# When and how densely a second list of rows is scattered to DRAM, in a two-layer encoder with product-key experts

## The chip, the cores and the metric

The kernel runs on one core of a Trainium2 chip. The metric is the device time of one execution in microseconds (us). The launch has two layers, and both run the same program on other weights.

## The reference

Each of the two layers adds a token mixer (two kinds of attention, gates, projections) and then a product-key expert layer to `x`, 256 tokens of 1024 numbers. The change touches only the expert layer:

```python
def peer_ffn(x, w_query, sub_keys, expert_down, expert_up):
    ...
        q = (xc @ w_query).reshape(PEER_CHUNK, PEER_HEADS, 2, half)
        s = jnp.einsum('thpk,pnk->thpn', q, sub_keys).astype(jnp.float32)
        sv, si = lax.top_k(s, PEER_TOPK)
        ...
        top_s, sel = lax.top_k(cand, PEER_TOPK)
        eidx = jnp.take_along_axis(cidx, sel, axis=-1)
        g = jax.nn.softmax(top_s, axis=-1)
        u = expert_down[eidx]
        vv = expert_up[eidx]
        act = jax.nn.gelu(jnp.einsum('td,thkd->thk', xc, u).astype(jnp.float32), approximate=False)
        return jnp.einsum('thk,thkd->td', (g * act).astype(x.dtype), vv)
```

Each token uses 8 heads x 16 of the 16,384 experts (128 x 128). The sum over `vv` needs only the rows of `expert_up` that some token uses.

## The kernel before, in words

**Stages of a layer.** Attention and projections come first. Then the expert layer has two long stages on TensorE. In the *downs* stage the kernel multiplies all 16,384 rows of `expert_down` with all 256 tokens: 128 units of 128 experts, two units to a PSUM bank (loop `b` from L1351 on, matmuls L1367 to L1369). Beside it VectorE finds the top 16, and gates are spread into a table `act`, which holds for each of 128 expert rows `i` (128 experts, one per partition) a row of 258 words: the gated activation for two halves of 128 tokens, and behind each half the expert's number. In the *ups* stage TensorE multiplies blocks of 128 rows of `expert_up` with those activations (`block`, matmuls L1401); three matmuls of 128x512 per half of the output and per half of the tokens, as weights and activations are both split into a high and a low part.

**Two lists and eight whole rows.** The expert rows are in three parts. List 1 (`r` = 0) holds the rows 0 to 79. The experts of it that are used are packed into 66 blocks of 128, of which 33 serve both token halves and 33 one half; they alternate. The rows 80 to 87 are taken whole, 8 units, without packing. List 2 (`r` = 1) holds the rows 88 to 127, packed into 33 blocks. The ups stage goes through list 1, the whole rows, list 2, 107 units.

**Packing takes four steps.** `rank_lane` computes each expert's place in its list (VectorE writes `rank`, L1178). `send_lane` then *sends* every row `i` of `act`: an indirect DMA from GpSimd (POOL) scatters its 128 x 258 words to their places in a DRAM table, `rows` (L1212): 80 sends for list 1, 40 for list 2. When all sends of a list are done, `read_back` brings blocks of 128 places back into SBUF by SP (L1243), into a ring of 16. And `rows` starts, from the expert numbers at the end of the block, an indirect DMA from POOL that *gathers* 128 rows of `expert_up`, 512 KB (L1272). The whole rows are loaded directly by SP (L1269).

**What a gathered unit passes through.** ScalarE copies it, rounded, to `wh` (L199), VectorE subtracts that from the original into `wl` (L203, the *split* of the unit, whose name is put in the list `st.splits`), and TensorE uses both. The raw buffers are a ring of `DEEP` = 10: 4 `raw`, 6 within `act`. A gather of unit n needs the split of unit n - 10; `wh` and `wl` have 4 buffers, so the split of unit n needs TensorE to be done with unit n - 4.

**What sets the order.** The kernel's Python simulates clocks of the engines (`Lanes`) and records instructions in the order in which lanes become ready; every engine then works its queue in that order. POOL and SP queues are in order too, so a send that waits holds back each gather behind it. `st.nd` counts the loads recorded so far, `up0` is the number of the layer's first ups unit, and `whole` is that of the first whole row.

**Pacing.** Each send is given a dependence on one entry of `st.splits`, so that the sends spread out in time: `pace` starts three entries before the end of the list and moves on by a step per send. While `pace` is past the end, the lane waits in the recording, up to 15 steps of 0.2 us of its own clock. For list 2 the lane waits besides until the first `DEEP` ups loads are recorded:

```python
            while r and st.nd < up0 + DEEP:
                yield None
            pace = len(st.splits) - 3.0
```

Of the kernel before, what the change touches and what calls it, by code (L numbers as in the profile page):

```python
# [58 lines left out]
DEEP = RAWS + AHEAD  # L59
# [167 lines left out]
def encoder_kernel(ctx, tc, x_in, wts, downs, ups, gains, gate_bias, qk_norm, rpb, sink, skeys, consts, sums, out,  # L227
# [8 lines left out]
    lanes = Lanes()  # L236
# [41 lines left out]
    def lane_need(keys):  # L278
        while not all(k in done for k in keys):
            yield None  # L280
        yield ("at", max(done[k] for k in keys))
# [71 lines left out]
    st = Stream(nc, wpool, srcs, lanes)  # L353
# [121 lines left out]
    for l in range(depth):  # L475
# [719 lines left out]
        def send_lane(r):  # L1195

            i0, w = LISTS[r][:2]
            yield from lane_need([("rank", r)])
            whole = up0 + len([x for x in seq if x[1] == 0])
            while r and st.nd < up0 + DEEP:  # L1200
                yield None
            pace = len(st.splits) - 3.0
            for i in range(i0, i0 + w):
                yield from lane_need([("row", i // 2)])

                tries = 0
                while int(pace) >= len(st.splits) and tries < 15 and lanes.stuck < 5:
                    tries += 1
                    yield ("w", 0.2)
                    yield ("p", 0.0)  # L1210

                snd = nc.gpsimd.indirect_dma_start(byrank[r], bass.IndirectOffsetOnAxis(ap=rank[:, i:i + 1], axis=0),  # L1212
                                                   afl[:, i * ROW:(i + 1) * ROW], None)
                key = f"send{l}{r}"
                if i > i0:
                    tc.declare_no_dep(snd.ins, group=key, reason="places of one list differ")
                tc.add_to_no_dep_group(key, snd.ins)
                tc.add_manual_dep(snd.ins, st.splits[min(int(pace), len(st.splits) - 1)],
                                  mybir.DependencyInfo(mybir.DependencyClass.Sync, mybir.DependencyReason.DATA),
                                  reason="pace")  # L1220

                pace += 0.4 if r == 0 else 1.8 if st.nd < whole else 0.6
                sends[r].append(snd.ins)
                nc.gpsimd.nop()
                yield ("w", 0.8)
                yield ("p", 0.0)
            sent.add((l, r))
            st.load(0)
# [101 lines left out]
        for r in range(len(LISTS)):  # L1330
            lanes.add(send_lane(r))
        stage, ring, sent, sends = {}, {}, set(), {r: [] for r in range(len(LISTS))}
        st.rows = rows
        up0 = u + 12 + 128
# [239 lines left out]
```

## Time and profile before

| | |
|---|---|
| time, median of 3 runs | 1810.36 us (1807.65 to 1810.52) |
| time of the profiled execution | 1814.21 us |
| its span, first to last instruction | 1812.4 us |
| PE busy | 1779.2 us, 98% of the span |
| DVE, ACT, POOL busy | 1439.7, 1096.0, 581.6 us |
| granted clock of PE, mean | 0.998 |
| DMA, mean | 208 GB/s |

The profile is of one execution, which is 3.85 us longer than the median of the runs. The span is 1.8 us shorter than that execution's own time. PE's busy time counts each matmul from its start to its modelled end, and neighbours overlap, so a count of matmuls in a stretch tells more of a pause than the busy time does. In layer 0 the ups stage begins at 673.93 us, in layer 1 at 1578.31 us.

### The profile page before, as it was taken

How to read it: one execution, taken by the hardware profiler on the slowest of the kernel's cores; microseconds unless marked ns; L12 is line 12 of the kernel's file. 1: busy time of each engine (PE TensorE's matmuls, PEld its weight loads, DVE VectorE, ACT ScalarE, POOL GpSimd, SP SyncE). 2: the span in 40 equal slices, each digit the busy share in tenths (PEclk: the TensorE clock that was granted, in tenths of full speed). 3: DMA queues.
4: the chain of work that ended last, by engine and by line, in shares of the span. 5: the costliest groups of instructions: out<-in, count | busy, mean ns of one | idle time of the engine just before them, and what ended most of it. 6: DMA issues, size and time to landing. Idle time of an engine off the chain costs nothing. (4 is left out here: it accounts for less than half of the span.)

```text
span 1812.4 us, 38043 instructions
## 1 busy us (share of the span) xinstructions
PE 1779.2 (98%) x14646; PEld 1632.9 (90%) x14646; DVE 1439.7 (79%) x3278; ACT 1096.0 (60%) x1788; POOL 581.6 (32%) x480
## 2 busy tenths in 40 slices
PE   8999999999999999989999999999999999999998
PEld 7889899999999998768878898999999999988786
DVE  6986799988878867656679867999888788677665
ACT  5675556666667646555656655556666676466554
POOL 0000260000047737775300002500000477377661
PEclk9999999999999999999999999999999999999999
DMA  7535456544468879999654354455444677899893
GB/s 260 161 112 171 150 164 186 165 151 148 147 187 243 244 254 319 297 318 320 215 204 150 110 176 153 156 186 172 148 145 152 187 244 240 262 326 334 307 333 131
DMA packets 130519, 377.42 MB, mean 208 GB/s; under 512 B 17552, under 2 KB 43792, under 8 KB 130320
## 3 DMA queue, kind: packets, MB, share of 16 engines
q1 hardware_dynamic: 90288, 239.28, 43.0%
q0 software_dynamic: 40032, 135.54, 20.8%
q8 instruction: 119, 1.95, 0.5%
q14 instruction: 80, 0.66, 0.1%
HBM read 342.00 MB, written 32.75 MB: 207 GB/s over the span
## 5 line engine op out<-in xcount | busy, mean ns | idle before, releaser
L203 DVE TENSOR_TENSOR wl<-raw,wh 128x1024 fp32r<-128x1024 f32 x444 | 541.6, 1222 | 150.3 <-ACT wh L199 142.2
L199 ACT ACTIVATE wh<-raw 128x1024 fp32r<-128x1024 f32 x476 | 502.5, 1057 | 226.5 <-PE bank L1368 53.8
L1367 PE MATMUL bank<-TT,wh 128*128 128x256 f32 x2048 | 592.0, 289 | 0.0
L1368 PE MATMUL bank<-TT,wh 128*128 128x256 f32 x2048 | 578.9, 283 | 0.0
L1369 PE MATMUL bank<-TT,wl 128*128 128x256 f32 x2048 | 578.4, 282 | 0.0
L1368 PEld LDWEIGHTS bank<-TT,wh 128*128 128x128 f32 x2048 | 392.1, 191 | 0.0
L1369 PEld LDWEIGHTS bank<-TT,wl 128*128 128x128 f32 x2048 | 391.8, 191 | 0.0
L1367 PEld LDWEIGHTS bank<-TT,wh 128*128 128x128 f32 x2048 | 391.5, 191 | 0.3
L1401 PE MATMUL bank<-wh,TT 128*128 128x512 f32 x1296 | 355.1, 393 | 10.6 <-ACT TT L1288 5.5
L1212 POOL DMA_INDIRECT rows<-act,rank x240 | 275.5, 1148 | 98.2 <-issue 61.3
L1401 PEld LDWEIGHTS bank<-wh,TT 128*128 128x128 f32 x1296 | 241.0, 188 | 73.1 <-DVE TT L1290 11.9
L888 POOL IOTA act<- 128x128 uint32 (+2 forms) x6 | 2.0, 332 | 891.7 <-PE bank L368 409.9
L203 DVE TENSOR_TENSOR wl<-act,wh 128x1024 fp32r<-128x1024 f32 x126 | 154.4, 1227 | 82.2 <-ACT wh L199 81.8
L1401 PE MATMUL bank<-wl,TT 128*128 128x512 f32 x648 | 201.6, 390 | 0.7 <-issue 0.7
L199 ACT ACTIVATE wh<-act 128x1024 fp32r<-128x1024 f32 x126 | 133.4, 1060 | 102.5 <-PE bank L1401 76.0
L1272 POOL DMA_INDIRECT act<-in_ups_dram,act x118 | 131.3, 1112 | 72.4 <-DVE TT L1290 27.4
L1401 PEld LDWEIGHTS bank<-wl,TT 128*128 128x128 f32 x648 | 122.0, 188 | 26.8 <-issue 1.1
L448 PE MATMUL bank<-TT,wh 128*128 128x256 f32 x448 | 130.1, 290 | 1.6 <-ACT raw_ka L577 1.0
L450 PE MATMUL bank<-TT,wh 128*128 128x256 f32 x448 | 126.6, 283 | 0.0
L451 PE MATMUL bank<-TT,wl 128*128 128x256 f32 x448 | 126.6, 283 | 0.0
L1272 POOL DMA_INDIRECT raw<-in_ups_dram,act x80 | 95.7, 1197 | 84.7 <-DMA act<-rows 54.6
L1072 ACT ACTIVATE oh<-oh 128x1024 f16<-128x1024 f16 (+2 forms) x108 | 101.4, 955 | 11.5 <-DVE oh L1069 10.4
(268 smaller groups left out, 2898.8 us busy)
## 6 DMA issues: line engine op xcount, KB each, us to landing
raw<-in_downs_dram SPq DMA_DIRECT2D x256, 512.0 KB, 3.8
raw<-in_wts_dram SPq DMA_DIRECT2D x132, 512.0 KB, 4.1
act<-rows SPq DMA_DIRECT2D x100, 129.0 KB, 5.0
act<-rows SPq DMA_DIRECT2D x98, 64.5 KB, 5.9
act<-in_ups_dram SPq DMA_DIRECT2D x8, 512.0 KB, 7.7
raw<-in_ups_dram SPq DMA_DIRECT2D x8, 512.0 KB, 5.3
rows<-act,rank POOLq DMA_INDIRECT x240
act<-in_ups_dram,act POOLq DMA_INDIRECT x118
```

The costliest lines, as they stand in the source:

```text
L199: self.nc.scalar.activation(h, r, AF.Copy)
L203: self.splits.append(engine.tensor_sub(lo, r, h.bitcast(F32)).ins.name)
L448: nc.tensor.matmul(o, wh, rh, start=first and i == 0 and pc == 0, stop=False, skip_group_check=True)
L450: nc.tensor.matmul(o, wh, rl, start=False, stop=False, skip_group_check=True)
L451: nc.tensor.matmul(o, wl, rh, start=False, stop=last and i == len(kcs) - 1 and pc == 1, skip_group_check=True)
L1072: nc.scalar.activation(el, ej, AF.Copy, scale=LOW)
L1212: snd = nc.gpsimd.indirect_dma_start(byrank[r], bass.IndirectOffsetOnAxis(ap=rank[:, i:i + 1], axis=0), afl[:, i * ROW:(i + 1) * ROW], None)
L1272: nc.gpsimd.indirect_dma_start(w, None, ups_rows, bass.IndirectOffsetOnAxis(ap=num, axis=0), element_offset=l * 16384 * D)
L1367: nc.tensor.matmul(o, lh, TT[:, :, 0, kc, :], start=kc == 0, stop=False)
L1368: nc.tensor.matmul(o, lh, TT[:, :, 1, kc, :], start=False, stop=False)
L1369: nc.tensor.matmul(o, ll, TT[:, :, 0, kc, :], start=False, stop=kc == 7)
L1401: nc.tensor.matmul(oacc[ch][hf], a, r[:, hf * 512:(hf + 1) * 512], start=first[hf] and a is lh and r is h, stop=last and a is ll)
```

## The change

It edits `send_lane` alone, and there only list 2:

- The wait until ten ups loads are recorded goes. The lane for list 2 records sends as soon as its places are known.
- `pace` starts six entries before the end of `st.splits`, not three, and a send may be tied at the latest to the fourth entry from the end (`lag` = 4), not to the last.
- The steps: 0.4 per send until two ups loads are recorded, then 2.8 (was 1.8) until the whole rows come, then 0.8 (was 0.6).

For list 1 the values come out as they were.

```diff
--- before.py
+++ after.py
@@ -1197,14 +1197,14 @@
             i0, w = LISTS[r][:2]
             yield from lane_need([("rank", r)])
             whole = up0 + len([x for x in seq if x[1] == 0])
-            while r and st.nd < up0 + DEEP:
-                yield None
-            pace = len(st.splits) - 3.0
+
+            lag = (1, 4)[r]
+            pace = len(st.splits) - (3.0, 6.0)[r]
             for i in range(i0, i0 + w):
                 yield from lane_need([("row", i // 2)])
 
                 tries = 0
-                while int(pace) >= len(st.splits) and tries < 15 and lanes.stuck < 5:
+                while int(pace) > len(st.splits) - lag and tries < 15 and lanes.stuck < 5:
                     tries += 1
                     yield ("w", 0.2)
                     yield ("p", 0.0)
@@ -1215,11 +1215,11 @@
                 if i > i0:
                     tc.declare_no_dep(snd.ins, group=key, reason="places of one list differ")
                 tc.add_to_no_dep_group(key, snd.ins)
-                tc.add_manual_dep(snd.ins, st.splits[min(int(pace), len(st.splits) - 1)],
+                tc.add_manual_dep(snd.ins, st.splits[min(int(pace), len(st.splits) - lag)],
                                   mybir.DependencyInfo(mybir.DependencyClass.Sync, mybir.DependencyReason.DATA),
                                   reason="pace")
 
-                pace += 0.4 if r == 0 else 1.8 if st.nd < whole else 0.6
+                pace += 0.4 if r == 0 or st.nd < up0 + 2 else 2.8 if st.nd < whole else 0.8
                 sends[r].append(snd.ins)
                 nc.gpsimd.nop()
                 yield ("w", 0.8)
```

On TensorE, VectorE and ScalarE the recorded order is the same in both kernels. POOL's queue moves. At the start of layer 0's ups stage it held this, where `rows_2244` is the DRAM table of list 1 and `rows_2245` that of list 2 (a send writes to it), and a DMA from `in_ups_dram` is a gather:

```order
L1212 DMA rows_2244<-act,rank 10240x258 x80
L1272 DMA raw<-in_ups_dram,act 128x1024 x4
L1272 DMA act<-in_ups_dram,act 128x1024 x6
L1272 DMA raw<-in_ups_dram,act 128x1024
L1212 DMA rows_2245<-act,rank 5120x258 x2
L1272 DMA raw<-in_ups_dram,act 128x1024
L1212 DMA rows_2245<-act,rank 5120x258
L1272 DMA raw<-in_ups_dram,act 128x1024 x2
L1272 DMA act<-in_ups_dram,act 128x1024 x2
L1212 DMA rows_2245<-act,rank 5120x258 x2
L1272 DMA act<-in_ups_dram,act 128x1024 x2
L1212 DMA rows_2245<-act,rank 5120x258
```

And now:

```order
L1212 DMA rows_2244<-act,rank 10240x258 x80
L1212 DMA rows_2245<-act,rank 5120x258 x9
L1272 DMA raw<-in_ups_dram,act 128x1024
L1212 DMA rows_2245<-act,rank 5120x258
L1272 DMA raw<-in_ups_dram,act 128x1024
L1212 DMA rows_2245<-act,rank 5120x258 x2
L1272 DMA raw<-in_ups_dram,act 128x1024
L1212 DMA rows_2245<-act,rank 5120x258
L1272 DMA raw<-in_ups_dram,act 128x1024
L1272 DMA act<-in_ups_dram,act 128x1024 x6
L1272 DMA raw<-in_ups_dram,act 128x1024 x2
```

Nine sends of list 2 moved ahead of the first gather, four more stand among the first four gathers, and behind them the sends stand further apart. Counting on to the 66th gather, the last of list 1, 33 sends of list 2 stand before it now and 32 before; seven and eight follow it. Layer 1 has the same counts at these places.

On SP, at the end of list 1 in layer 0, whole rows (L1269), blocks read back (L1243, from `rows_2245` those of list 2) and the next layer's gains (L1448) stood so:

```order
L1243 DMA act<-rows_2244 128x129
L1269 DMA act<-in_ups_dram 128x1024 x4
L1269 DMA raw<-in_ups_dram 128x1024 x2
L1243 DMA act<-rows_2245 128x258
L1243 DMA act<-rows_2245 128x129
L1269 DMA raw<-in_ups_dram 128x1024
L1243 DMA act<-rows_2245 128x258
L1269 DMA raw<-in_ups_dram 128x1024
L1448 DMA act<-in_gains_dram 128x1024
L1243 DMA act<-rows_2245 128x129
L1243 DMA act<-rows_2245 128x258
```

And now:

```order
L1243 DMA act<-rows_2244 128x129
L1269 DMA act<-in_ups_dram 128x1024 x4
L1269 DMA raw<-in_ups_dram 128x1024 x4
L1448 DMA act<-in_gains_dram 128x1024
L1243 DMA act<-rows_2245 128x258
L1243 DMA act<-rows_2245 128x129
L1243 DMA act<-rows_2245 128x258
L1243 DMA act<-rows_2245 128x129
L1243 DMA act<-rows_2245 128x258
```

The last two whole loads and the gains moved ahead of the first read-back of list 2, which waits for all its sends. In layer 1 the whole loads move alike, and there are no gains.

## Rows read from the trace of the kernel before

**Rows 1.** The page, first part: busy us (share of the span) and instructions.
```profile
PE 1779.2 (98%) x14646; PEld 1632.9 (90%) x14646; DVE 1439.7 (79%) x3278; ACT 1096.0 (60%) x1788; POOL 581.6 (32%) x480
```

**Rows 2.** Stages: length, busy us (and instructions) per engine, PEclk, DMA share, GB/s.
```profile
580.00:600.00 20.00, 20.00 (x260) 19.79 (x259) 17.70 (x39) 14.19 (x22) 15.73 (x15) 1.00 0.81 227
640.00:660.00 20.00, 20.00 (x175) 19.80 (x174) 12.60 (x22) 8.55 (x11) 1.18 (x1) 1.00 0.61 188
720.00:740.00 20.00, 20.00 (x90) 16.57 (x89) 14.22 (x21) 12.73 (x21) 15.67 (x15) 1.00 0.96 335
760.00:780.00 20.00, 18.75 (x75) 13.11 (x75) 11.18 (x16) 9.29 (x15) 15.74 (x14) 1.00 0.89 279
780.00:800.00 20.00, 17.84 (x74) 12.96 (x73) 11.71 (x17) 10.25 (x16) 15.73 (x15) 1.00 0.90 290
800.00:820.00 20.00, 17.91 (x69) 11.98 (x68) 12.43 (x18) 10.97 (x17) 12.93 (x11) 1.00 0.74 291
1700.00:1720.00 20.00, 18.71 (x78) 14.05 (x77) 13.32 (x19) 11.73 (x19) 11.95 (x12) 1.00 0.76 278
```

**Rows 3.** Timeline of PE, ups stages (start us, us, instruction, [idle before <-releaser]).
```profile
673.93 0.63 PE L1401 MATMUL bank<-wh 128*128 128x512 f32 x2
...
690.01 1.07 PE L1401 MATMUL bank<-wh,TT 128*128 128x512 f32 x4
...
691.37 1.07 PE L1401 MATMUL bank<-wh,TT 128*128 128x512 f32 x4
...
1578.31 0.63 PE L1401 MATMUL bank<-wh 128*128 128x512 f32 x2
```

**Rows 4.** Timeline of ACT: the copies of ups units.
```profile
697.46 1.06 ACT L199 ACTIVATE wh<-act 128x1024 fp32r<-128x1024 f32 x1 [1.35 <-PE bank L1401]
...
744.54 1.06 ACT L199 ACTIVATE wh<-act 128x1024 fp32r<-128x1024 f32 x1 [0.94 <-DMA act<-in_ups_dram,act]
...
814.45 1.06 ACT L199 ACTIVATE wh<-act 128x1024 fp32r<-128x1024 f32 x1 [0.50 <-DMA act<-in_ups_dram,act]
...
823.40 1.06 ACT L199 ACTIVATE wh<-raw 128x1024 fp32r<-128x1024 f32 x1 [1.35 <-PE bank L1401]
...
1718.64 1.06 ACT L199 ACTIVATE wh<-raw 128x1024 fp32r<-128x1024 f32 x1 [1.35 <-PE bank L1401]
```

**Rows 5.** Timeline of POOL, layer 0: sends (L1212) and gathers (L1272).
```profile
633.03 0.96 POOL L1212 DMA_INDIRECT rows<-act,rank  x1 [0.30 <-issue]
658.82 1.68 POOL L1272 DMA_INDIRECT raw<-in_ups_dram,act  x1 [24.84 <-DMA act<-rows]
...
665.92 0.94 POOL L1272 DMA_INDIRECT raw<-in_ups_dram,act  x1 [1.93 <-DMA act<-rows]
667.16 0.94 POOL L1272 DMA_INDIRECT act<-in_ups_dram,act  x1 [0.30 <-DMA act<-rows]
...
686.30 0.94 POOL L1272 DMA_INDIRECT act<-in_ups_dram,act  x1 [0.30 <-issue]
...
737.67 1.02 POOL L1272 DMA_INDIRECT act<-in_ups_dram,act  x1 [0.30 <-DMA act<-rows]
...
758.03 1.96 POOL L1212 DMA_INDIRECT rows<-act,rank  x1 [0.30 <-DMA act<-rows]
...
802.75 1.49 POOL L1272 DMA_INDIRECT act<-in_ups_dram,act  x1 [0.30 <-issue]
...
816.17 1.43 POOL L1212 DMA_INDIRECT rows<-act,rank  x1 [0.30 <-issue]
822.50 1.46 POOL L1272 DMA_INDIRECT act<-in_ups_dram,act  x1 [4.90 <-DVE TT L1290]
```

**Rows 6.** Timeline of DVE: list 2's places, and one subtraction.
```profile
642.32 0.19 DVE L1178 CAST rank<-scr 128x40 uint32<-128x40 f32 x1
...
757.90 1.23 DVE L203 TENSOR_TENSOR wl<-raw,wh 128x1024 fp32r<-128x1024 f32 x1 [0.80 <-ACT wh L199]
```

**Rows 7.** Timeline of SP: the first read-back of list 2.
```profile
819.40 0.80 SPq L1243 DMA_DIRECT2D act<-rows  x2
```

## The prediction

> **What bounds the kernel now.** I began with the page: TensorE (PE) is busy for 1779.2 of 1812.4 us [rows 1], so nothing can be won except where it pauses, and its own matmuls are untouched. "Busy" counts the pipelined tail of a matmul, so I looked for pauses in the stage table by 20 us, by the count of matmuls. Layer 0's ups stage runs at 90 matmuls per 20 us at 720 us, but at 75, 74 and 69 from 760 to 820 us; in layer 1 only 1700 to 1720 us falls, to 78 [rows 2]. The granted clock is 1.00 in all these rows, so it is not the clock.
>
> How late is PE? One block for one half of the tokens is six matmuls, and two neighbouring groups start 1.36 us apart (690.01 and 691.37) [rows 3]. List 1 has 33 blocks for both halves and 33 for one, 99 groups or 134.6 us. Begun at 673.93 us it should end at 808.6, and the first whole unit, two groups, at 811.3. ScalarE's copy of the fifth whole unit waits for exactly that end, since `wh` has four buffers. Unpaused, such a copy starts 0.4 us after PE is done (697.46 us, against 697.05 by the same count for unit 10); the fifth whole unit's starts at 823.40 us [rows 4]. So PE is 823.40 - 0.4 - 811.3 = 11.7 us late. Layer 1 begins at 1578.31 [rows 3] and has its copy at 1718.64 [rows 4]: 2.6 us late. Together **14.3 us**, the most this change can give back.
>
> Who is late? ScalarE's copy at 744.54 us is the first that waits for a gather [rows 4]: the gather of unit 37, which POOL began at 737.67, 6.9 us earlier [rows 5]. (I number units from the first block of list 1, and write P(n) for PE's unpaused start on unit n: 673.93 + 4.08 per pair, the second of a pair 2.72 later.) POOL itself does not wait then: its rows stand 0.30 us apart, with "issue" or a long-done transfer before them [rows 5]. From the gather of unit 14 (686.30) to that of unit 37 (737.67) POOL issues 23 gathers and 14 sends, 37 instructions in 51.4 us, **1.39 us** each. PE needs a unit every 2.04 us, and 37/23 x 1.39 = 2.24 us of POOL goes into one. POOL is the slower, and its lead is used up. From unit 37 to 65 (802.75) it is 43 instructions in 65.1 us, 1.51 each. To be in time a gather must begin 6.9 us (landing) + 1.06 (copy) + 1.23 (subtraction) = 9.2 us before P(n) [rows 4, 6]. For unit 37 that is 740.9, met; for unit 65 798.0, missed by 4.8 us. The last gather also lands 11.7 us after its issue (814.45) [rows 4], with SP loading whole units beside it. So POOL's instructions between gathers set the pauses.
>
> **The change, step by step.** On TensorE, VectorE and ScalarE the instructions and their order stay; only POOL's queue moves, and four transfers on SP.
>
> *Nine sends ahead of the first gather.* POOL is idle from 633.03 + 0.96 to 658.82 us, where the first gather waits for a read-back [rows 5]. List 2's places are known at 642.5 [rows 6]. Nine sends at 1.39 us take 12.5 us and end at 655.0, inside the gap: nothing on the path. Their split ties reach at least four entries back, to splits done earlier, since splits run ahead of PE; their rows of `act` have long been written. Their bytes meet a DMA share of 0.61, and at 580 to 600 us sends ran at 15 per 20 us beside the same loads, share 0.81, with PE at 20.00 of 20 [rows 2].
>
> *Four sends among the first four gathers.* They put 4 x 1.39 = 5.6 us before the gather of unit 4, less the 1.93 us that the gather of unit 3 already waits for its read-back: 667.16 + 3.6 = 670.8 us [rows 5]. P(4) - 9.2 = 672.9. Spare 2.1 us, the thinnest place. The bounds for this step are nothing, and 1 us of pause per layer if landing is slower; I take 0.5 per layer.
>
> *Fewer sends between later gathers.* Counting POOL's order: before the gather of unit 33 stand, after the first gather, 33 + 12 = 45 instructions (47 before); of unit 50, 68 (74); of unit 65, 89 (97). From 660.7 us (the first gather and 1.9 for the read-back) at 1.39 us they begin at 723.3, 755.2 and 784.4; needed are 732.7, 766.7 and 798.0. At 1.51 us they would be at 728.7, 763.4 and 795.1, still in time. The lead breaks at (798.0 - 660.7) / 89 = 1.54 us. The 11.7 us go, and layer 1's 2.6 by the same count.
>
> A rule speaks against a fixed price. The send at 758.03 us took 1.96 us, begun 0.13 us after a VectorE subtraction at 757.90; that at 633.03 took 0.96 [rows 5, 6]. The Trainium skill ("SBUF — State Buffer", Who interferes with whom) says that a VectorE instruction with two SBUF inputs contends with a GpSimd instruction that reads SBUF, and that the later one fully blocks. The row agrees; the sum by a fixed 1.39 us would then hold only while POOL keeps out of step with the subtractions, and a gather freed by one would be long.
>
> *The tail of list 2.* Its last seven sends follow the gather of unit 65. Before, the last eight took from 804.2 to 817.6 us, 1.67 each, SP's read-back began at 819.40 and the first gather of list 2 at 822.50 [rows 5, 7]. P(74) is 808.6 + 8 x 2.72 = 830.3, so that gather is needed by 821.1. If the gather of unit 65 ends at 796.5 at the latest and the wider tie stretches the seven in the ratio 0.8 to 0.6, 2.2 us each, they end at 811.9, and the 4.9 us from the last send to the gather make 816.8: in time. On SP the last two whole loads now stand ahead of the read-back, and the load of the next gains too; the whole loads were not late before and a direct issue is short, so both cost nothing. If the pauses go, the opening is the next thing to be late.
>
> *Sum.* 11.7 + 2.6 - 1.0 = 13.3 us. The profiled execution took 1814.21 us, so 1800.9. It stands 3.85 us above the median, 1810.36; if that excess lies in the same pauses, the time is 1800.9 in any run; if it is spread over the kernel, 1797.1. I take the middle, **1799 us**.
>
> **Rivals.**
> *The transfers are the bound, not POOL.* For it: DMA share 0.96 at 720 to 740 us. Against: it is 0.89 and 0.90 in the paused rows, with POOL busy 15.7 of 20 us [rows 2]. Then only bytes count: eight fewer sends between the first and the last gather, 8 x 132,096 bytes, at 280 GB/s 3.8 us in layer 0, and at most 2.6 in layer 1. Time 1804 to 1808, say 1806. Chance 0.12.
>
> *The early sends fall in step with the subtractions.* At 1.96 + 0.30 = 2.26 us each, nine end at 642.5 + 20.3 = 662.8, 4.0 us past the first gather; four more add 9.0 less 1.9: unit 4's gather comes at 667.16 + 11.1 = 678.3, 5.4 us late, 10.8 for both layers, and the same long instructions leave a few us of the old pauses: 1810, no change. Against: 15 instructions in 15.73 us at 580 us, 1.05 each [rows 2]. Chance 0.07. This is the port rule of the Trainium skill's SBUF page taken to its end.
>
> *The sends hold back the gathers: slower.* POOL's queue is in order. If the ties or the waits for `act` rows keep the nine until 658.8, 13 sends (18.1 us, less 1.9) stand before the gather of unit 4: 683.4 us, 10.5 late, 21 us for both layers, less the 14.3 that then no longer arise: 1810.4 + 6.7 = 1817 us. It decides when the ninth send ends after 660.9 us (2.1 spare), and costs more than it saves from about 668. For it: the tie is to a split whose time the trace does not show for these sends. Against: four splits of age. Chance 0.09.
>
> **How the numbers follow.** Forecast 0.72, rivals 0.12, 0.07 and 0.09. The forecast's own range is 1796 (all 14.3 us off the median) to 1803; with the transfers' case the range is 1795.5 to 1808, which leaves out the last two. About 0.2% (3.6 us) can be told from no change, so faster is below 1806.7: 0.72 + 0.09 of the transfers' 0.12 = 0.81; same 0.03 + 0.07 = 0.10; slower 0.09.
>
> **What would show it.** Right: nine sends on POOL from about 642.5 to 655 us, the first gather still near 658.8, the gather of unit 65 near 785 to 795, 88 to 90 matmuls in every 20 us from 680 to 820, and POOL idle before some gathers until a buffer is free. Wrong: ScalarE still waiting for gathers at 745 us with POOL gaps above 0.30 us (transfers), or a pause of PE at 680 to 690 (opening), or the first gather of list 2 later than P(74) - 9.2.

## The result, and the profile after

The changed kernel takes **1801.55 us** in the median of 6 runs (1798.99 to 1804.93). The kernel before took 1810.36 on the same chip (1807.65 to 1815.02; one disturbed run of it is left out). The ratio of the runs is put at 0.9943, 95% interval [0.9922, 0.9964]; that of the two medians is 0.9951. So it is faster by about half a percent. The profiled execution took 1798.99 us, span 1797.2, 15.2 us less than the one before. Two numbers are to be explained: 15.2 us between two executions, and about 9 us between medians.

The page after, first part, against [rows 1]:

```profile
PE 1771.5 (99%) x14646; PEld 1634.2 (91%) x14646; DVE 1438.8 (80%) x3278; ACT 1096.4 (61%) x1788; POOL 577.5 (32%) x480
```

The stage table after, columns as in [rows 2]:

```profile
640.00:660.00 20.00, 20.00 (x175) 19.80 (x175) 12.76 (x22) 8.55 (x12) 12.46 (x9) 1.00 0.77 233
720.00:740.00 20.00, 20.00 (x90) 16.57 (x89) 14.22 (x21) 12.72 (x21) 15.64 (x15) 1.00 1.01 358
760.00:780.00 20.00, 20.00 (x90) 16.56 (x89) 14.61 (x20) 12.72 (x20) 15.47 (x15) 1.00 1.00 368
800.00:820.00 20.00, 20.00 (x90) 16.57 (x89) 13.54 (x18) 11.80 (x18) 9.43 (x8) 1.00 0.96 319
1700.00:1720.00 20.00, 20.00 (x90) 16.58 (x89) 12.39 (x16) 10.59 (x16) 10.03 (x11) 1.00 0.90 309
```

The rows that held 75, 69 and 78 matmuls are at 90, and the other rows of list 1 at 89 or 90. From 640 to 660 us POOL has 9 instructions in place of one: the early sends. The last two columns belong to the question of the bound: from 720 to 780 us the DMA share is now 1.00 to 1.01 at 358 to 368 GB/s, where the paused row at 760 us had 0.89 at 279. So 279 was not what the transfers can do.

The timeline of PE after, the two starts of the ups stage, and that of ScalarE: two copies that wait for a gather in the openings, and the copy of the fifth whole unit in each layer:

```profile
674.15 0.63 PE L1401 MATMUL bank<-wh 128*128 128x512 f32 x2
1565.46 0.63 PE L1401 MATMUL bank<-wh 128*128 128x512 f32 x2
```
```profile
683.53 1.06 ACT L199 ACTIVATE wh<-act 128x1024 fp32r<-128x1024 f32 x1 [0.87 <-DMA act<-in_ups_dram,act]
811.96 1.06 ACT L199 ACTIVATE wh<-raw 128x1024 fp32r<-128x1024 f32 x1 [1.35 <-PE bank L1401]
1575.05 1.06 ACT L199 ACTIVATE wh<-act 128x1024 fp32r<-128x1024 f32 x1 [1.74 <-DMA act<-in_ups_dram,act]
1703.73 1.06 ACT L199 ACTIVATE wh<-raw 128x1024 fp32r<-128x1024 f32 x1 [1.35 <-PE bank L1401]
```

From the start of the stage to that copy are 137.81 us in layer 0 (before 823.40 - 673.93 = 149.47) and 138.27 in layer 1 (before 140.33) [rows 3, 4]: 11.66 and 2.06 us less, 13.7 together. That is where the prediction said the time lay. Of the other 1.5 us, 1.4 lie between that copy in layer 0 and the start of layer 1's ups stage (1578.31 - 823.40 = 754.91 us before, 1565.46 - 811.96 = 753.50 now); what they are was not followed up.

POOL after, layer 0, against [rows 5]: the last send of list 1, the first and last of the nine early sends, the gathers of units 0, 4, 14, 37, 64 and 65, the last send, and the first gather of list 2:

```profile
633.25 0.96 POOL L1212 DMA_INDIRECT rows<-act,rank  x1 [0.30 <-issue]
643.58 2.00 POOL L1212 DMA_INDIRECT rows<-act,rank  x1 [9.37 <-ACT wh L199]
...
657.52 0.96 POOL L1212 DMA_INDIRECT rows<-act,rank  x1 [0.30 <-issue]
660.61 0.97 POOL L1272 DMA_INDIRECT raw<-in_ups_dram,act  x1 [2.13 <-DVE wl L203]
...
671.91 0.95 POOL L1272 DMA_INDIRECT act<-in_ups_dram,act  x1 [0.30 <-issue]
...
688.91 1.05 POOL L1272 DMA_INDIRECT act<-in_ups_dram,act  x1 [0.30 <-issue]
...
732.37 1.13 POOL L1272 DMA_INDIRECT act<-in_ups_dram,act  x1 [0.31 <-issue]
...
782.15 1.66 POOL L1272 DMA_INDIRECT act<-in_ups_dram,act  x1 [1.16 <-DVE TT L1290]
...
785.42 1.13 POOL L1272 DMA_INDIRECT act<-in_ups_dram,act  x1 [0.30 <-issue]
...
795.03 1.04 POOL L1212 DMA_INDIRECT rows<-act,rank  x1 [0.30 <-issue]
807.48 1.18 POOL L1272 DMA_INDIRECT act<-in_ups_dram,act  x1 [11.41 <-DVE wl L203]
```

The gather of unit 65 begins at 785.42 us (before 802.75). The one of unit 64 waits 1.16 us for VectorE, and the first one of list 2 waits 11.41 us for the split that frees its buffer: POOL is ahead now.

### The profile page after: what moved, and what is told of

It reads as the page before. It is cut to its first block, busy times and chain, and to the rows that moved or that the text cites. A ratio compares the mean times of both kernels' runs of the same rounds, so it can differ in the third digit from the quotient of the medians.

```text
span 1797.2 us, 38047 instructions
## 1 busy us (share of the span) xinstructions
PE 1771.5 (99%) x14646; PEld 1634.2 (91%) x14646; DVE 1438.8 (80%) x3278; ACT 1096.4 (61%) x1788; POOL 577.5 (32%) x480
## 5 line engine op out<-in xcount | busy, mean ns | idle before, releaser
L1401 PE MATMUL bank<-wh,TT 128*128 128x512 f32 x1296 | 349.2, 390 | 3.4 <-DVE TT L1290 2.2
L1212 POOL DMA_INDIRECT rows<-act,rank x240 | 278.1, 1159 | 114.7 <-issue 60.3
L1272 POOL DMA_INDIRECT act<-in_ups_dram,act x118 | 130.8, 1108 | 89.4 <-DVE TT L1290 36.7
L1072 ACT ACTIVATE oh<-oh 128x1024 f16<-128x1024 f16 (+2 forms) x108 | 101.4, 955 | 11.5 <-DVE oh L1069 10.4
L1109 ACT ACTIVATE act<-bank 128x288 f32<-128x288 f32 (+31 forms) x152 | 52.2, 347 | 92.0 <-PE bank L1096 87.8
```

The lines of the kernel that those rows point to most:

```text
L1072: nc.scalar.activation(el, ej, AF.Copy, scale=LOW)
L1272: nc.gpsimd.indirect_dma_start(w, None, ups_rows, bass.IndirectOffsetOnAxis(ap=num, axis=0), element_offset=l * 16384 * D)
L1401: nc.tensor.matmul(oacc[ch][hf], a, r[:, hf * 512:(hf + 1) * 512], start=first[hf] and a is lh and r is h, stop=last and a is ll)
```

## The experiments

The theory: POOL's instructions between gathers set the pauses, and the wider steps take them out. The rivals: the transfers are the bound, and only fewer bytes helped; or the early start is what helped. I give each kernel's ratio to the kernel before, run on the same chip; it differs a little from the ratio of the medians, as above. Three numbers are read from the timelines of POOL and ScalarE in layer 0: POOL's instructions from the gather of unit 14 to that of unit 37 (23 units, 23 x 2.04 = 46.9 us of PE) with the mean us from one start to the next, and the **lead**, from the start of a gather to ScalarE's copy of that unit.

| kernel | instructions, us each | lead at unit 4, 14, 37, 54 | ratio |
|---|---|---|---|
| before | 37, 1.388 | 11.3, 11.2, 6.9, 6.3 | 1 |
| changed | 32, 1.358 | 6.8, 8.8, 11.6, 15.6 | 0.9943 [0.9922, 0.9964] |
| early_only | 37, 1.358 | 8.0, 11.5, 7.5, 7.0 | 0.9998 [0.9989, 1.0007] |
| thin_only | 32, 1.357 | 11.3, 12.8, 15.7, 17.0 | 0.9962 [0.9948, 0.9976] |
| burst_old_steps | 36, 1.501 | 5.6, 6.9, 7.3, 5.8 | 1.0155 [1.0135, 1.0175] |
| half_gather_bytes | 37, 1.358 | 11.3, 11.5, 7.5, 7.4 | 0.9942 [0.9926, 0.9957] |
| pool_count_back | 38, 1.432 | 6.1, 7.1, 5.2, 5.5 | 1.0177 [1.0156, 1.0199] |
| bytes_back | 32, 1.352 | 6.2, 8.6, 11.6, 15.6 | 0.9971 [0.9954, 0.9988] |
| gap_repeat | 32, 1.357 | 11.3, 12.9, 15.7, 16.9 | 0.9946 [0.9933, 0.9959] |

### One part of the change at a time

**early_only** drops the old wait and keeps the old steps and ties.

```diff
-            while r and st.nd < up0 + DEEP:
-                yield None
```

> Only the wait for ten ups loads is dropped; tie and steps stay as they were (1.8, 0.6). Four sends come before the first gather, but the old spacing puts 33 between the first gather and that of unit 65 (32 before): 98 POOL instructions instead of 97. Theory (POOL's count between gathers sets the pauses): nothing gained, 1808 to 1812 us, pauses of layer 0 still 9 to 14 us. Rival (it is the early start that helps, as the sends then run in an idle stretch): part of the gain, about 1805 us. Transfers as the bound: 33 sends of bytes instead of 32, no change.

Measured 1807.62 us (before there 1807.1): no change. Stage table; POOL, gathers of units 37 and 65; and in layer 0 the start of the stage (PE) and the copy of the fifth whole unit (ScalarE):

```profile
760.00:780.00 20.00, 20.00 (x90) 16.58 (x89) 14.54 (x20) 12.76 (x19) 15.73 (x15) 1.00 0.95 315
780.00:800.00 20.00, 17.71 (x78) 14.16 (x77) 11.58 (x16) 9.54 (x16) 16.04 (x14) 1.00 0.96 345
```
```profile
736.27 1.11 POOL L1270 DMA_INDIRECT act<-in_ups_dram,act  x1 [0.31 <-issue]
...
798.19 0.94 POOL L1270 DMA_INDIRECT act<-in_ups_dram,act  x1 [0.30 <-issue]
```
```profile
673.99 0.63 PE L1399 MATMUL bank<-wh 128*128 128x512 f32 x2
816.36 1.06 ACT L199 ACTIVATE wh<-raw 128x1024 fp32r<-128x1024 f32 x1 [1.35 <-PE bank L1399]
```

PE pauses late, from about 780 us on. From start to copy are 142.37 us, against the 137.81 of the changed kernel: layer 0 is 4.6 us late, and layer 1, read in the same way (1571.66 to 1713.03 us), 3.6. That is less than the 9 to 14 that I had expected and less than the 11.7 of [rows 3, 4], so the profiled execution of before, 1814.21 us, is a poor measure of the usual pause: this one took 1808.97 us, and its kernel's median is that of before. By the count, 98 instructions from the first gather to that of unit 65 (97 before), nothing was to be gained, and nothing was.

**thin_only** is the change with the old wait put back.

```diff
+            while r and st.nd < up0 + DEEP:
+                yield None
```

> The changed kernel with the old wait for ten ups loads put back: no send ahead of the first gather, old ties replaced and steps 2.8 and 0.8. 21 sends stand before the gather of unit 65 and 19 after it. Theory (count): 86 POOL instructions to unit 65, its gather at about 781 us and no pause in list 1; but list 2's sends end 26 to 42 us later, at 809 to 824, and its first gather at 820 to 835 where 821 is needed: 0 to 14 us of a new pause per layer, before list 2; 1797 to 1828 us, I say 1812. Rival (early start alone helps): list 1's pauses stay as before, 1810 us.

Measured 1800.57 us, ratio 0.9962: without the early start, the wider spacing gives the gain, and the rows of list 1 stand at 90. The older ties are in this kernel too. That they give the gain was not tested on a chip like this one; but in the kernel before no send was held by its tie: from 678 to 803 us in layer 0 and from 1580 to 1702 us in layer 1 every instruction of POOL begins 0.30 or 0.31 us after the end of the one ahead of it. The pause in the tail that I had expected did not come: with 19 sends behind the gather of unit 65, two copies of list 2 wait for a gather, but PE runs 90 matmuls from 820 to 840 us all the same.

The two again, on one chip, beside the three kernels further down:

> The changed kernel itself, for a comparison on one chip with the next three. The wider spacing alone was at 0.9962 [0.9948, 0.9976] of the kernel before. If the early start adds nothing, this is within 1 us of the wider spacing alone in the next run (some 1800 to 1802 us where the kernel before is at 1807); if the early start is worth what the ratios 0.9943 and 0.9962 suggest, it is 3 us below it.

> The wider spacing alone (old wait until ten loads are recorded), repeated beside the whole change. Both theories: no pauses of PE in list 1. Early start adds nothing: the same time as the whole change within 1 us. Early start is worth something: 3 us longer than the whole change, with the difference in the tail of list 2 (800 to 840 us), where 19 sends follow the gather of unit 65.

Measured 1802.35 us (1798.9 to 1806.36), ratio 0.9961 [0.9943, 0.9979], for the whole change, and 1800.57 (1800.03 to 1801.8), 0.9952 [0.9937, 0.9968], for the spacing alone. The intervals overlap: the early start adds nothing that can be told. But the spread of the whole change is 7.5 us, of the spacing alone 1.8. In this execution of the whole change the gather of unit 4 began at 673.40 us, and five copies of layer 0's opening waited for gathers. The 672.9 us of the prediction belong to a stage that begins at 673.93; here it began at 674.36, so that gather was needed by 673.3. The loss stayed small, and after the copy of unit 13 no copy of list 1 waited again (start of the stage, and copy of the fifth whole unit):

```profile
674.36 0.63 PE L1401 MATMUL bank<-wh 128*128 128x512 f32 x2
812.55 1.06 ACT L199 ACTIVATE wh<-raw 128x1024 fp32r<-128x1024 f32 x1 [1.35 <-PE bank L1401]
```

That is 138.19 us, 0.4 more than the 137.81 of the first execution.

**burst_old_steps** starts early with step 0.4, and then keeps the old steps and ties.

```diff
-            while r and st.nd < up0 + DEEP:
-                yield None
...
-                pace += 0.4 if r == 0 else 1.8 if st.nd < whole else 0.6
+                pace += 0.4 if r == 0 or st.nd < up0 + 2 else 1.8 if st.nd < whole else 0.6
```

> Wait dropped and the early step of 0.4 kept, so nine sends come before the first gather as in the changed kernel, but the later steps are the old ones (1.8, 0.6) and the tie is the old one. POOL instructions from the first gather to that of units 33, 50, 65: 51, 78, 96 (before 47, 74, 97; changed 45, 68, 89). Theory (count): at 1.40 us unit 50's gather comes at 769.8 where 766.7 is needed, so pauses stay, 5 to 12 us in layer 0: 1804 to 1811 us. Rival (early start alone): as the changed kernel, 1799 to 1803 us. Transfers as the bound: 31 sends of bytes instead of 32, no gain, 1810 us.

Measured 1834.16 us, ratio 1.0155: a miss, more than 20 us above what I expected. The count to unit 65 is 96, one less than before, but the lead is only 5.6 us at unit 4 (before 11.3), ScalarE waits for gathers from unit 3 on, PE loses its first matmuls between 700 and 720 us (84 in place of 90), and the loss grows from there. Stage table and POOL, gathers of units 4, 50 and 65:

```profile
720.00:740.00 20.00, 18.62 (x77) 13.50 (x75) 11.59 (x16) 10.40 (x17) 15.73 (x15) 1.00 0.94 297
```
```profile
673.32 1.31 POOL L1270 DMA_INDIRECT act<-in_ups_dram,act  x1 [0.30 <-issue]
...
777.71 0.96 POOL L1270 DMA_INDIRECT raw<-in_ups_dram,act  x1 [0.30 <-DMA act<-rows]
...
804.70 1.02 POOL L1270 DMA_INDIRECT act<-in_ups_dram,act  x1 [0.30 <-issue]
```

Two things follow. Every gather has its own due time, and PE does not regain what it lost: unit 50 was due at 766.7 and is 11 us late, while unit 65, due at 798.0, is 6.7 late. And while PE pauses, an instruction of POOL costs 1.50 us, not 1.36.

### Bytes or instructions

**half_gather_bytes** is the kernel before, with gathers of 512 words instead of 1024; the first half of a row stands for both, so the products of list 1 and list 2 are other ones.

```diff
-                nc.gpsimd.indirect_dma_start(w, None, ups_rows, bass.IndirectOffsetOnAxis(ap=num, axis=0),
+                nc.gpsimd.indirect_dma_start(w[:, 0:UNIT // 2], None, ups_half, bass.IndirectOffsetOnAxis(ap=num, axis=0),
```

> The kernel before, with every gather fetching 512 instead of 1024 words of a row (the first half is used twice, so the ups products of gathered units are other ones); POOL's instructions and their order are unchanged. Theory (POOL's count): POOL still issues without a gap above 0.30 us from 680 to 800 us at 1.38 to 1.51 us each, the gather of unit 65 at 795 to 803; pauses shrink only by the shorter landing (by 1 to 3 us, and the last by up to 6), so 3 to 8 us late in layer 0: 1798 to 1806 us. Transfers as the bound: POOL waits for free buffers from about 700 us, the gather of unit 65 before 785, no pause: 1796 us or below.

Measured 1797.17 us (1796.52 to 1797.96), ratio 0.9942, and no pause, where my theory had left 3 to 8 us of it. This seemed to speak for the transfers. But POOL's queue is that of before, at 1.358 us each, and the lead falls from 11.5 to 7.5 us as there; only it is enough now. Stage table, DMA issues from 680 to 820 us (last number: median us from issue to landing), and POOL, units 37 and 65:

```profile
760.00:780.00 20.00, 20.00 (x90) 16.58 (x89) 14.53 (x20) 12.74 (x20) 15.43 (x16) 1.00 0.73 200
```
```profile
act<-in_ups_dram,act POOLq DMA_INDIRECT x35, 4.0
```
```profile
736.38 1.13 POOL L1280 DMA_INDIRECT act<-in_ups_dram,act  x1 [0.30 <-issue]
...
794.92 1.07 POOL L1280 DMA_INDIRECT act<-in_ups_dram,act  x1 [0.30 <-issue]
```

A gather lands in 4.0 us here; the one of unit 37 before took the 6.9 us of [rows 4, 5]. So bytes count through the landing of one gather: the lead must exceed it. Whether they count through the rate of all, the next two ask.

**pool_count_back** gives the changed kernel POOL instructions without bytes, **bytes_back** bytes without POOL instructions:

```diff
+                if 12 <= k < 66 and k % 4 == 0:
+                    nc.gpsimd.indirect_dma_start(extra_[:, 2 * k - 24:2 * k - 16], None, ups_few,
+                                                 bass.IndirectOffsetOnAxis(ap=num, axis=0),
+                                                 element_offset=l * 16384 * D)
```
```diff
+                if 12 <= k < 66 and k % 4 == 0:
+                    nc.sync.dma_start(spill_[32 * k - 384:32 * k - 256, :], cst[:, 0:ROW])
```

> The whole change, and behind every fourth gather of list 1 from the 13th to the 65th a second gather of 128 x 8 words from the same numbers, never used: 14 more POOL instructions with 4 KB each, so POOL has 103 instructions between the first gather and that of unit 65 (89 in the change, 97 before) and the transfers carry what they carry in the change. POOL's count is the bound: 103 x 1.39 us put the gather of unit 65 at about 804, 6 us too late, and the pauses of before come back: 1808 to 1820 us. The transfers are the bound: no pauses, 1800 to 1802 us. Both: up to 1806.

> The whole change, and behind every fourth gather of list 1 from the 13th to the 65th a direct transfer by SP of 128 x 258 words from a constant in SBUF to a DRAM table that nothing reads: 14 times 132,096 bytes, more than the eight sends that left this stretch, and no POOL instruction. POOL's count is the bound: the gather of unit 65 stays near 785 us and no pauses come, 1800 to 1803 us. The transfers are the bound: the pauses of before come back, 1807 to 1815 us, with POOL at 15 instructions per 20 us, none of them waiting, and ScalarE waiting for gathers that were begun in time.

Measured 1838.65 us, ratio 1.0177, for 14 more instructions per layer, and 1801.66 us, 0.9971, for 14 times 132,096 bytes. Stage table of pool_count_back, and its gathers of units 4, 37 and 65:

```profile
760.00:780.00 20.00, 16.34 (x66) 11.32 (x65) 11.31 (x15) 10.49 (x16) 15.73 (x15) 1.00 0.89 269
```
```profile
673.39 1.29 POOL L1274 DMA_INDIRECT act<-in_ups_dram,act  x1 [0.30 <-issue]
...
745.99 1.12 POOL L1274 DMA_INDIRECT act<-in_ups_dram,act  x1 [0.31 <-issue]
...
813.91 1.90 POOL L1274 DMA_INDIRECT act<-in_ups_dram,act  x1 [0.30 <-issue]
```

And the start of its stage in layer 0, with the copy of the fifth whole unit:

```profile
674.33 0.63 PE L1407 MATMUL bank<-wh 128*128 128x512 f32 x2
831.02 1.06 ACT L199 ACTIVATE wh<-raw 128x1024 fp32r<-128x1024 f32 x1 [1.35 <-PE bank L1407]
```

Stage table of bytes_back, and its gather of unit 65:

```profile
720.00:740.00 20.00, 20.00 (x90) 16.57 (x89) 14.22 (x20) 12.73 (x21) 15.47 (x15) 1.00 1.04 378
760.00:780.00 20.00, 20.00 (x90) 16.56 (x89) 14.22 (x21) 12.84 (x20) 15.43 (x16) 1.00 1.02 381
```
```profile
784.97 1.12 POOL L1273 DMA_INDIRECT act<-in_ups_dram,act  x1 [0.31 <-issue]
```

In this execution of bytes_back, with a DMA share of 1.02 to 1.04 at 378 to 381 GB/s, PE runs 90 matmuls in every row from 700 to 820 us, an instruction of POOL costs 1.352 us and the lead at unit 37 is 11.6 us, as in the change. So that rate of transfers does not bring the pauses back by itself; more instructions on POOL do. But only six of its eleven runs, this one among them, lie at 1797.12 to 1801.66 us. The other five, at 1806.65 to 1809.19, are as long as the kernel before (1808.5). None of them was profiled: that the added bytes cost time there, through the opening, which is as thin as the change's, or otherwise, is not excluded.

The size of pool_count_back is a miss, nearly 20 us above the expectation. Its opening is that of the other execution of the change: the gather of unit 4 begins at 673.39 us (673.40 there), and the stage 674.33 (674.36). There 0.4 us were lost, here layer 0 is 831.02 - 674.33 - 137.81 = 18.9 us late. PE has 86 matmuls from 680 to 700 us, 90 again from 700 to 720, and then pauses in every row up to 820 (granted clock 0.91 in the last of them, 1.00 in the others). What differs is the count behind the opening, and while PE pauses every instruction costs more: the 103 take 813.91 - 661.49 = 152.4 us, 1.48 each, where I had counted with 1.39.

### A version without the thin place

**gap_only** sends either before the first load of the stage or after the tenth, none between.

```diff
+                if r and up0 <= st.nd < up0 + DEEP:
+                    while st.nd < up0 + DEEP:
+                        yield None
+                    pace = len(st.splits) - 6.0
```

It ran twice, as the first time its chip took 1957.94 us for the kernel before. Two others ran there with it: **tie_only**, the kernel before with the older ties alone, and **step_2_0**, thin_only with 2.0 for 2.8.

> Only the tie moves (pace starts six entries back, ties reach at most the fourth entry from the end); the old wait and the old steps 1.8 and 0.6 stay, and POOL's queue is word for word that of before (32 sends before the gather of unit 65). The count on POOL is the bound: no change, 1806 to 1810 us, pauses of PE from 760 to 820 us. A send held by its tie delays the gathers: then a younger tie cost something before, and this would be 2 to 10 us faster with POOL rows that wait no longer for a subtraction.

> The wider spacing alone with a step of 2.0 in place of 2.8: 29 sends before the gather of unit 65 (32 before, 21 with 2.8), 12 of them between the gathers of units 14 and 37 and 14 from there to unit 65. In the runs without pauses POOL issues in step with PE at 1.358 us per instruction, three per pair of units (4.08 us); so one send per pair keeps the lead, more uses it up. Theory of the count: 35 x 1.358 = 47.5 us for 23 units against PE's 46.9, then 42 x 1.358 = 57.0 against 57.1: the lead from gather to copy falls by about 0.6 us from some 11.5 and stays near 10, above the landing of 5 to 9 us: no pauses, 1800 to 1802 us, as with 2.8. If the whole width of the step is needed (the lead must grow): pauses near the end of list 1, 1803 to 1807.

> The whole change, but sends of list 2 are recorded either before the first load of the stage (six here) or after the tenth, none among the first ten gathers; the steps of the change stay. 27 sends before the gather of unit 65. The opening of the whole change is its thinnest place: the gather of unit 4 at 671.9 to 673.4 us against 672.9 needed, and PE lost some matmuls at 680 to 700 us in one of its two profiled executions. If that is what is left, this one has the gather of unit 4 near 669 us, 90 matmuls in every 20 us, and 1799 to 1801 us with runs closer together (within 3 us) than the whole change's (1798.9 to 1806.4). If the opening is not it: 1801 to 1803 and the same spread.

On that chip tie_only took 1959.17 us (ratio 1.0003 [0.9979, 1.0026]), step_2_0 1955.8 (0.9996 [0.9969, 1.0022]) and gap_only 1934.77 (0.9865 [0.9831, 0.9898]). The kernel loses its time elsewhere too on that chip. Stage table from 500 to 600 us, first of tie_only there, whose POOL queue is that of before, then of the kernel before on its first chip:

```profile
500.00:600.00 100.00, 84.00 (x918) 78.83 (x917) 60.31 (x134) 50.96 (x82) 50.45 (x48) 0.91 0.56 170
500.00:600.00 100.00, 98.03 (x1254) 96.81 (x1253) 83.12 (x183) 70.45 (x111) 65.30 (x59) 1.00 0.73 219
```

PE has 918 matmuls at a granted clock of 0.91 in place of 1254 at 1.00, and the transfers 170 in place of 219 GB/s; why was not found. So these three decide nothing about the chips of the other runs: whether a step of 2.0 would do stays open, and for the ties alone there are only the rows of the kernel before, in which no send was held.

> The sends only in the gap ahead of the first load and behind the tenth, again, because the chip of the run before took 1958 us for the kernel before (its DMA moved less), so its times do not stand beside the others. On a chip that takes 1805 to 1812 us for the kernel before: if the opening is what is left of the whole change, the gather of unit 4 comes near 669 us, ScalarE's copies of units 4 to 13 wait for no gather, 90 matmuls stand in every 20 us of list 1, and the time is 1799 to 1801 us with runs within 3 us of each other (whole change 1798.9 to 1806.4, wider spacing alone 1800.0 to 1801.8). If the opening is not it: 1801 to 1803 us and a spread of 5 us or more.

Measured 1798.9 us (1798.14 to 1800.42), ratio 0.9946 [0.9933, 0.9959]. POOL, the gathers of units 4 and 65, and the stage table:

```profile
666.17 0.94 POOL L1276 DMA_INDIRECT act<-in_ups_dram,act  x1 [0.30 <-DMA act<-rows]
...
784.19 1.12 POOL L1276 DMA_INDIRECT act<-in_ups_dram,act  x1 [0.30 <-issue]
```
```profile
680.00:700.00 20.00, 20.00 (x90) 16.57 (x89) 15.36 (x21) 13.13 (x20) 15.43 (x16) 1.00 0.98 336
```

No copy of list 1 waits for a gather in either layer, and the runs lie within 2.3 us. Of the kernels that fetch all their bytes it has the lowest median and, with thin_only, the closest runs, but on another chip, and its ratio is not told apart from that of the change.

## Why the prediction was right, step by step

**The pauses: right.** 11.7 and 2.6 us were to go, less 0.5 in each opening: 11.2 and 2.1. They gave 11.66 and 2.06. Layer 0's opening lost less than I took. Both are differences to one execution of before whose pauses were longer than usual, as the last point here says.

**Nine sends in the gap: the place was right, the price low.** They began at 643.58 us and ended at 658.48, not 655.0. Four of the nine took 1.77 to 2.00 us. The first gather slid by 1.8 us to 660.61, but POOL stood idle for 2.13 us before it, so the sends did not hold it on POOL; what did was not followed up. They ended 2.4 us ahead of the 660.9 at which the slower rival begins. In the runs the early start bought nothing (early_only, thin_repeat): I had priced it as nothing on the path, and so it is, but I had not said that the change does not need it.

**The opening: right that it is the thinnest place.** Forecast 670.8 us for the gather of unit 4, due 672.9; measured 671.91 in one execution and 673.40 in another, due 673.1 and 673.3 by the starts of their stages. The lead at unit 4 is 6.0 to 6.8 us, against 11.3 where no sends stand there, and in gap_repeat, on its chip, the spread is gone with it. burst_old_steps and pool_count_back show the other side: where the count behind the opening is also above what PE's pace allows, the lead does not recover, and the loss grows until the kernel is 27 to 30 us slower than before. So sends that crowd the opening can make the kernel slower, as the slower rival had it; the wider steps keep the change from it.

**The count: right.** Units 33, 50 and 65 were to begin at 723.3, 755.2 and 784.4 us; they began at 724.23, 755.56 and 785.42. For unit 65 the agreement is in part luck: POOL waits for VectorE at unit 64 (1.16 us, and that gather takes 1.66), so there PE's pace and not the price of an instruction sets the time. pool_count_back shows that it is the count.

**The price of an instruction: the number was near, its meaning was not.** I took 1.39 us and feared 1.51. Where PE does not pause it is 1.352 to 1.358 us, in six of the kernels of the table, and 3 x 1.358 = 4.07 us is PE's period for two units, 4.08. So with two gathers and one send per two units POOL keeps pace; before there were 37 instructions for 11.5 periods, 3.2 in each, now 2.8. The 1.51 us that I read between units 37 and 65 was no price of its own but what the pauses make of it: half_gather_bytes, with the same queue and no pause, issues the same 43 instructions at 1.36. step_2_0, which was to lie between 2.8 and 3.2, ran only on the chip where nothing was decided, so the count at which the lead begins to shrink is worked out from the price and not measured.

**The tail: right side, wrong price.** I stretched the last sends to 2.2 us by the ties; they came every 1.3 to 1.5 us, and the first gather of list 2 came at 807.48 us, not 816.8.

**The rivals.** Against the transfers as the bound speak pool_count_back, where 14 instructions of 4 KB each bring the pauses back, the row from 760 to 780 us, which moved 279 GB/s with pauses and 368 without, and the profiled execution of bytes_back; its five longer runs are not explained. Sends that meet subtractions are a true mechanism of the wrong size: four of the nine early sends were long by it, and in the steady part POOL meets subtractions too, but with little of them left (last section).

**The sum: mis-sized in one term.** Between the two profiled executions 13.3 us were forecast for the pauses and 13.7 came. What failed is the step from there to the runs: I took the middle between two readings of the 3.85 us by which the profiled execution of before exceeded its median. Between the medians 11.4 us were forecast and 8.8 came. The pauses of that execution were longer than usual: half_gather_bytes, with no pauses, stands 9.9 us below the median of before on its chip (1807.1), not 14.3, and early_only, as long as before in the median, lost 8.1 us to pauses in its profiled execution. So the excess lay in the pauses, the first reading (1800.9) was the better one, and 1799 was 2.5 us too low.

## What to carry to other kernels

Where one queue feeds a steady engine, count its instructions per period of that engine: what matters is whether the lead of the feed grows or shrinks, and the lead at each item, not only at the last, since the fed engine did not regain a pause in any of these runs. Put extra work of that queue in its idle gap or spread it below the break-even count, and never where the lead is smallest. And a price read behind the first pause is not the price that holds when there is none. One profiled execution can be untypical: compare what it loses with the spread of the runs before a forecast is built on it.

## What the runs showed of the hardware that I had not expected

**An indirect DMA on POOL waits for the rest of a subtraction on VectorE.** In step, the kernel before at 690 us, and out of step, at 745 us; VectorE first, then POOL:

```profile
690.39 1.29 DVE L203 TENSOR_TENSOR wl<-raw,wh 128x1024 fp32r<-128x1024 f32 x1 [1.16 <-ACT wh L199]
...
745.64 1.23 DVE L203 TENSOR_TENSOR wl<-act,wh 128x1024 fp32r<-128x1024 f32 x1 [0.78 <-ACT wh L199]
```
```profile
690.42 0.99 POOL L1212 DMA_INDIRECT rows<-act,rank  x1 [0.30 <-issue]
...
745.83 1.86 POOL L1272 DMA_INDIRECT raw<-in_ups_dram,act  x1 [0.30 <-issue]
```

The one at 745.83 begins 0.19 us into a subtraction that has 1.04 us left, and takes 1.04 + 0.82. The one at 690.42 begins 0.03 us in, takes 0.99, and the subtraction takes 1.29 instead of 1.23. From 680 to 800 us (803 in the kernel before) the same was read for eight kernels, those of the table without early_only. 415 instructions began at least 0.06 us into a subtraction with at least 0.1 us of it left, and each took that remainder plus 0.80 to 0.89 us. The 226 that met none took 0.97 in the mean; 7 that began in its first 0.04 us took 0.94 to 1.00, and it took 1.27 to 1.30. The Trainium skill ("SBUF — State Buffer", Who interferes with whom) says that a VectorE instruction with two SBUF inputs contends with a GpSimd instruction that reads SBUF, and calls the shared port pair an exclusive lock. The 415 agree; the 7, which came later than the subtraction and were not held, do not follow it.

It explains 1.36 against 1.50 us. While PE does not pause, two subtractions come close together in each period (772.25 and 773.61 us in the changed kernel, the next at 776.33) and leave the rest of it free; when it pauses, they lie apart. In the kernel before, 20 of the 39 instructions between 744 and 803 us met one with 0.64 us left in the mean, against 18 of 38 with 0.31 between 686 and 738. From 680 to 800 us an instruction takes 1.06 us in the mean in half_gather_bytes and 1.20 in burst_old_steps, and with the 0.30 us to the next one these are the two prices.

**A feed that lost its step and has too many instructions stays slow.** In burst_old_steps 36 instructions for 23 units cost POOL 54.0 us at 1.501 each. At 1.358 they would have cost 48.9, only 2.0 more than PE's 46.9: a shortfall of 2 us became one of 7. With 32 instructions in their place the second execution of the changed kernel found its step again after a late opening: 1.363 us each between units 14 and 37.
